# Two-layer hybrid encoder on one core: other buffers for the first feed-forward weights, block sums queued behind the last tile's eviction, row means on ScalarE

## The chip, the core and the metric

The kernel runs on one NeuronCore of a Trainium2 chip. The core has five engines with queues of their own: TensorE (PE, matrix products into PSUM), VectorE (DVE), ScalarE (ACT), GpSimd (POOL) and SyncE (SP, which here only issues transfers). The metric is the time of one execution in device microseconds, the median of several executions. The profile is one further execution with the hardware profiler on.

## The reference, cut to what matters

Two layers over 1024 tokens of width 1024, all in float32:

```python
for l in range(DEPTH):                       # DEPTH = 2
    h = _rmsnorm(x, g_pre_mix[l])
    z = h @ w_in[l]
    ...                                      # Fourier, windowed attention and memory groups -> y_f, y_a, y_m
    y = concat([rms(y_f), rms(y_a), rms(y_m)]) @ w_out[l]
    x = x + _rmsnorm(y, g_post_mix[l])
    h = _rmsnorm(x, g_pre_ffn[l])
    gate, up = jnp.split(h @ w_ffn_in[l], 2, axis=-1)      # D_FF = 2816
    f = (jax.nn.silu(gate) * up) @ w_ffn_out[l]
    x = x + _rmsnorm(f, g_post_ffn[l])
```

`_rmsnorm(x, g)` is `x * rsqrt(mean(x*x) + 1e-6) * g`, row by row.

## The kernel before, in words

**Products.** A float32 product is made of three products of split operands: `split` (L151, L152) rounds a block to a high part on ScalarE and takes the low part, source minus high part, on VectorE (or GpSimd); TensorE then multiplies high by high, high by low and low by high. Tokens are worked on in 8 tiles of 128 rows.

**The seam between attention and feed-forward.** The second half of the attention (`att_units(1)`), the output product and both norms are woven tile by tile in one loop over `i` (it runs to `NT + 4`). For tile `t`, `out` (L1030 to L1045) multiplies the tile by `w_out` (products `mo`, L162), evicts each half of 512 columns from PSUM on VectorE with the scale of its group (L1041), then calls `residual` and `norm_x`: the square with its row sum on ScalarE (L335), the row mean and its power -1/2 on GpSimd (L210, L212), scale and gain on VectorE (L337), the sum into `x` on VectorE (L338), then square (L289), mean and power on GpSimd again, and scale and gain on VectorE (L294). `Blocks.tile` transposes the normed tile on TensorE (`hTp`, L1066) and copies it out of PSUM on ScalarE (L1067).

**The feed-forward's first product** runs as one level of Strassen's scheme: seven block products, numbered 1 to 7, in the order 2, 4, 5, 1, 6, 7, 3. The token operands are blocks of 512 tokens by 512 columns, b11, b21 (tiles 0 to 3) and b12, b22 (tiles 4 to 7), and their sums: 2 and 4 need tiles 0 to 3 alone, the others tiles 4 to 7 as well. `Blocks.sum(n, c)` makes one quarter of the operand of product n: for 1, 4 and 6 a sum on VectorE (L1084), then in each case a split. `Blocks.last(c)` overwrites b21 and b12 with the sums (L1096, L1097) of which 7 and 3 are made. The weights come in quads: a `Quad` loads two blocks of `w_ffn_in` (512 KB each, L1112, on SP), `weights(i)` makes the operand of product i (for 1, 2, 5, 6 and 7 a sum on VectorE, L1127, then a split), and `step(i)` issues its 12 matmuls (L1137, results `qy`, `qz`, `qx`, `qw`) and the combinations. A gate quad and an up quad form a pair; there are 11 pairs in each layer. The steps of the first pair stand in the layer's loop, those of the others in `ffn_in`. Each layer ends with the second product `ffn_out` (`fo`, L1272), and the last tiles' norm.

**Buffers.** SBUF is two arenas, one for split operands and one for plain float32, with slots of 256 columns given by number. Rings of slot numbers (`qws` for quad weights, `sns` for copies of products, `wsums` for weight sums, `xfs` for the x and f of a tile) are reset at each seam. In the seam the x and f of tiles 5, 6 and 7 lie at 32 and 0, 16 and 20, 24 and 28, the attention's probabilities at 36 to 47, the two gains at 48 and 52.

**Order.** Each engine works through its queue in order. The order is fixed when the kernel is built: the framework goes through the instructions in the order in which the program names them and places them by a timeline model of its own, so that an instruction named later can be queued ahead of one that this model expects to wait. `tc.issue_after(ins)` makes every instruction in its block that runs on the engine of `ins` queue behind `ins`.

Of the kernel before, what the change touches and what calls it, by code (L numbers as in the profile page):

```python
# [15 lines left out]
AF = mybir.ActivationFunctionType  # L16
ALU = mybir.AluOpType
# [3 lines left out]
D = 1024  # L21
S = 1024
NT = S // P
# [3 lines left out]
FW = 256  # L27
# [7 lines left out]
EPS = 1e-6  # L35
# [31 lines left out]

@with_exitstack
def tile_encoder(ctx: ExitStack, tc: tile.TileContext, T, C, out):
    nc = tc.nc  # L70

# [10 lines left out]
    def nm(s):  # L82
        uid[0] += 1
        return f"{s}_{uid[0]}"
# [36 lines left out]
    def run(k, n, step):  # L121
        return Ring(*[k + i * step for i in range(n)])
# [7 lines left out]
    qws, sns, silus, acts = Ring(32, 0, 16, 20), Ring(36, 38, 40, 42, 32, 34), run(8, 5, 2), run(18, 7, 2)  # L130
    sums, wsums = run(8, 4, 2), Ring(4, 6)
# [6 lines left out]
    def sm(n, name="v"):  # L138
        if name not in smp:
            smp[name] = ctx.enter_context(tc.tile_pool(name="sm_" + name, bufs=N_SM.get(name, 4)))  # L140
        return smp[name].tile([P, n], F32, tag=name, name=nm(name))

    def ps(shape, name="ps", tag="pd"):
        return psp[tag].tile([P] + list(shape), F32, tag=tag, name=nm(name))
# [24 lines left out]
    def cst(*shape):  # L169
        n = math.prod(shape)  # L170
        ap = const[:, used[0] : used[0] + n]
        used[0] += -(-n // 8) * 8
        names = "abc"[: len(shape)]
        dims = {c: d for c, d in zip(names, shape)}
        return ap.rearrange(f"p ({' '.join(names)}) -> p {' '.join(names)}", **dims) if len(shape) > 1 else ap
# [4 lines left out]
    nc.vector.memset(ones, 1.0)  # L180
    mhalf = cst(8)
    nc.vector.memset(mhalf, -0.5)
    halfpi = cst(1)
    nc.vector.memset(halfpi, math.pi / 2)

# [4 lines left out]
        out=mask[:, 0:P], in_=mask[:, 0:P], pattern=[[1, P]], compare_op=ALU.is_ge,  # L190
# [4 lines left out]
        out=mask[:, 2 * P : 3 * P], in_=mask[:, 2 * P : 3 * P], pattern=[[-1, P]],  # L195
# [5 lines left out]
    rx = cst(NT)  # L201
# [2 lines left out]
    CC = cst(NT, HD // 2)  # L204
    SS = cst(NT, HD)

    def rsqrt_mean(ss, n, width, name="rs"):

        v = sm(width, name + "v")
        nc.gpsimd.tensor_scalar(out=v, in0=ss, scalar1=1.0 / n, scalar2=EPS, op0=ALU.mult, op1=ALU.add)  # L210
        r = sm(width, name)
        nc.gpsimd.tensor_tensor(out=r, in0=v, in1=mhalf[:, 0:width], op=ALU.pow)  # L212
        return r

    def gain(row, g):
# [70 lines left out]
    def norm_x(x, g, h=None, keep=None):  # L286

        ss = sm(1, "nss")
        nc.scalar.activation(junks(D // 2).bitcast(BF16) if h is None else h, x, AF.Square, accum_out=ss)  # L289
        if keep is not None:  # L290
            nc.scalar.dma_start(keep, x)
        h = x if h is None else h
        r = rsqrt_mean(ss, D, 1, "nrs")
        nc.vector.scalar_tensor_tensor(out=h, in0=x, scalar=r[:, 0:1], in1=g, op0=ALU.mult, op1=ALU.mult)  # L294
        return h

    def token_scale(x, t):

        ss = sm(1, "nss")
        nc.scalar.activation(junks(D // 2).bitcast(BF16), x, AF.Square, accum_out=ss)  # L300
        v = sm(1, "nrsv")
        nc.gpsimd.tensor_scalar(out=v, in0=ss, scalar1=1.0 / D, scalar2=EPS, op0=ALU.mult, op1=ALU.add)
        nc.gpsimd.tensor_tensor(out=rx[:, t : t + 1], in0=v, in1=mhalf[:, 0:1], op=ALU.pow)

    def norm_T(h, hT, t, tag="pd"):

# [13 lines left out]
    def residual_out(x, f, g, dst, t):  # L320

        ss = sm(1, "rss")
        nc.scalar.activation(junks(D // 2).bitcast(BF16), f, AF.Square, accum_out=ss)  # L323
        r = rsqrt_mean(ss, D, 1, "rrs")
        for n in range(2):
            ns = slice(n * 512, n * 512 + 512)
            nc.vector.scalar_tensor_tensor(out=f[:, ns], in0=f[:, ns], scalar=r[:, 0:1], in1=g[:, ns], op0=ALU.mult, op1=ALU.mult)
            (nc.gpsimd if t in (1, 3) else nc.vector).tensor_tensor(out=x[:, ns], in0=x[:, ns], in1=f[:, ns], op=ALU.add)
            (nc.sync, nc.scalar)[n].dma_start(dst[:, ns], x[:, ns])

    def residual(x, f, g, eng=None):

        junk = junks(D // 2).bitcast(BF16)
        ss = sm(1, "rss")
        nc.scalar.activation(junk, f, AF.Square, accum_out=ss)  # L335
        r = rsqrt_mean(ss, D, 1, "rrs")
        nc.vector.scalar_tensor_tensor(out=f, in0=f, scalar=r[:, 0:1], in1=g, op0=ALU.mult, op1=ALU.mult)  # L337
        (eng or nc.vector).tensor_tensor(out=x, in0=x, in1=f, op=ALU.add)  # L338

# [146 lines left out]
    class Mix:  # L486
# [57 lines left out]
        def fourier_units(self):  # L544

            v = nc.vector
# [18 lines left out]
            def products(r):  # L565
                th, tl, dh, dl = st.pop(("d", r))
                pt = ps([256], "yfp", "sc")
                acc = Acc(pt, 2)
                for i in range(2):
                    acc.add(th[:, i], tl[:, i], dh[:, i], dl[:, i])  # L570
                y = yfs(256)
                ss = sm(1, "fss")
                nc.scalar.activation(y, pt, AF.Square, accum_out=ss)
                rs = rsqrt_mean(ss, FW, 1, "frs")
                nc.scalar.activation(y, pt, AF.Copy, scale=rs[:, 0:1])
                st["y", r] = y

# [452 lines left out]
        def out(self, t, x1):  # L1030

            x, f = self.xf.pop(t)
            (hi, lo), rs = self.prepped.pop(t)
            for n in range(2):
                ns = slice(n * 512, n * 512 + 512)
                pt = ps([512], "mo")
                acc = Acc(pt, 4)
                for i in range(4):
                    w = self.woa[2 + i]
                    acc.add(hi[:, i], lo[:, i], w[0][:, ns], w[1][:, ns])  # L1040
                nc.vector.scalar_tensor_tensor(  # L1041
                    out=f[:, ns], in0=pt, scalar=rs[:, 0:1], in1=f[:, ns], op0=ALU.mult, op1=ALU.add
                )
            residual(x, f, self.gpost)
            return norm_x(x, self.gffn, f, x1)  # L1045
# [130 lines left out]
    def gate_out(q):  # L1176
        res = []
        for c in q.out:
            s = silus(512)
            nc.scalar.activation(s, c, AF.Silu)  # L1180
            res.append(s)
        return res
# [23 lines left out]
    def quads(l, p, hb):  # L1206
        return [Quad(l, j * DFF + 2 * p * P, hb) for j in range(2)]

    def ffn_in(l, hb, actd, first):

        for p in range(NFF // 2):
            if p == 0:
                gq, uq = first
                g = gate_out(gq)
                up_out(uq, g, actd, p)
                qws.ks, wsums.ks, sns.ks = (44, 48, 52, 56), (4, 6, 0, 2), (36, 38, 40, 42, 32, 34)
                continue
            gq, uq = quads(l, p, hb)
            for q in (gq, uq):
                q.load()  # L1220
                for i in ORDER:
                    q.step(i)
                if q is gq:
                    g = gate_out(gq)
            up_out(uq, g, actd, p)
# [121 lines left out]
    mix = Mix(0, hT, mem)  # L1347
# [13 lines left out]
    for l in range(DEPTH):  # L1361
# [4 lines left out]
        q = mix.skewed(mix.q, mix.q_turn, NT)  # L1366
# [8 lines left out]
        hb = Blocks()  # L1375
        hs = {}
        first = gq, uq = quads(l, 0, hb)
        qws.ks, wsums.ks, sns.ks = (32, 0, 16, 20), (4, 6), (36, 38, 40, 42, 56, 58)
        for r in (qws, wsums, xfs, sns, silus, acts, sums, wcs):
            r.i = 0  # L1380
        mix.values_32()
# [1 line left out]
        for i in range(NT + 4):  # L1383
            if i < NT + SKEW:
                att[i]()
            if 2 <= i < NT + 2:
                hs[i - 2] = mix.out(i - 2, x1d[i - 2])
            if i >= 4:
                hb.tile(hs.pop(i - 4), i - 4)
            if 1 <= i < NT + 1:  # L1390
                mix.out_rows(i - 1, xs[i - 1], pmd[i - 1])
            if 5 <= i < 9:
                hb.sum(2, i - 5)
            if i == NT + 1:
                gq.load()
                gq.step(2)
                for c in range(4):
                    hb.sum(4, c)
            if i == NT + 2:
                gq.step(4)  # L1400
                uq.load()
                uq.step(2)
                uq.step(4)
            if i > NT:
                for c in (i - NT - 1,) if i < NT + 3 else (2, 3):
                    hb.sum(5, c)
        for q in first:
            q.step(5)
        for n in (1, 6, 7, 3):
            for c in range(4):  # L1410
                hb.sum(n, c)
                if n == 6:
                    hb.last(c)
            for q in first:
                q.step(n)
        ffn_in(l, hb, actd, first)
# [4 lines left out]
        if l + 1 < DEPTH:  # L1421
            mem = Memory(l + 1, 16, 0, 16, 28, "pT")
            mix = Mix(l + 1, nhT, mem)
# [83 lines left out]
```

## Time and profile before

| | us |
|---|---|
| median of 3 runs | 2080.04 (2077.87 to 2081.79) |
| the profiled execution | 2080.67 |
| its span, first to last instruction | 2078.9 |
| PE busy | 1996.4 |
| DVE busy | 1572.7 |
| ACT busy | 1071.5 |
| POOL busy | 714.1 |
| mean granted TensorE clock | 0.981 of full speed |

A row of a group of instructions in the profile names the line, the engine, the operation, output and inputs by the program's names, partitions by elements and the count; behind the bar stand the busy time in us, the mean of one in ns, and the idle time of the engine in front of them with what ended it. A row of a timeline begins with start and length in us, and shows in brackets how long the engine was idle before and which engine's line ended that. In the chain of waits each row is start, length and what the end of the span waited for at that moment. Times within the span count from its start.

### The profile page before, as it was taken

How to read it: one execution, taken by the hardware profiler on the slowest of the kernel's cores; microseconds unless marked ns; L12 is line 12 of the kernel's file. 1: busy time of each engine (PE TensorE's matmuls, PEld its weight loads, DVE VectorE, ACT ScalarE, POOL GpSimd, SP SyncE). 2: the span in 40 equal slices, each digit the busy share in tenths (PEclk: the TensorE clock that was granted, in tenths of full speed). 3: DMA queues.
4: the chain of work that ended last, by engine and by line, in shares of the span. 5: the costliest groups of instructions: out<-in, count | busy, mean ns of one | idle time of the engine just before them, and what ended most of it. 6: DMA issues, size and time to landing. Idle time of an engine off the chain costs nothing.

```text
span 2078.9 us, 28540 instructions
## 1 busy us (share of the span) xinstructions
PE 1996.4 (96%) x9587; PEld 1646.8 (79%) x9587; DVE 1572.7 (76%) x2540; ACT 1071.5 (52%) x2270; POOL 714.1 (34%) x819
## 2 busy tenths in 40 slices
PE   7998999799999999999999989998999999999998
PEld 6876787588888888887888768876888888878886
DVE  5668767898787886768876687679887787778766
ACT  7467777554333333545555677686433333345451
POOL 5344445433333433002423544453442342320012
PEclk9999999899999999999999999998999999999999
DMA  6112132423232333879741122233233233269983
GB/s 222 45 48 67 61 102 96 158 67 106 96 115 94 115 103 115 304 267 327 273 153 49 57 67 77 78 123 130 97 117 101 87 132 97 97 210 342 302 274 141
DMA packets 173347, 286.48 MB, mean 138 GB/s; under 512 B 15464, under 2 KB 73360, under 8 KB 173200
## 3 DMA queue, kind: packets, MB, share of 16 engines
q1 hardware_dynamic: 165136, 265.78, 38.4%
q10 hardware_dynamic: 8064, 18.88, 2.4%
q8 instruction: 75, 1.23, 0.2%
q14 instruction: 72, 0.59, 0.1%
HBM read 218.02 MB, written 66.58 MB: 137 GB/s over the span
## 4 chain that ended last, share of the span: by engine, by line
PE 79%; DVE 7%; DMA 5%; ACT 3%; issue 2%; POOL 2%; SPq 0%; DVEq 0%; POOLq 0%; ACTq 0%
PE fo L1272 14%; PE qx L1137 11%; PE qz L1137 11%; PE qy L1137 11%; PE mo L162 7%; PE qw L1137 6%; PE kvp L162 4%; PE qp L162 3%; DVE arena_r L152 2%; DMA arena_f<-actd 2%; PE pT L798 2%; PE zT L162 2%; PE sc L761 2%; DMA arena_f<-in_w_ffn_out 1%; PE av L813 1%
## 5 line engine op out<-in xcount | busy, mean ns | idle before, releaser
L151 ACT CAST arena_r<-arena_f 128x512 fp32r<-128x512 f32 (+1 forms) x780 | 443.8, 591 | 646.4 <-PE qz L1137 114.0
L152 DVE TENSOR_TENSOR arena_r<-arena_f,arena_r 128x512 fp32r<-128x512 f32 (+1 forms) x676 | 509.4, 775 | 146.3 <-ACT arena_r L151 136.4
L1272 PE MATMUL fo<-arena_r 128*128 128x512 f32 x1848 | 426.5, 392 | 8.1 <-ACT arena_r L151 6.9
L1272 PEld LDWEIGHTS fo<-arena_r 128*128 128x128 f32 x1848 | 347.9, 189 | 82.0 <-ACT arena_r L151 5.7
L1137 PE MATMUL qy<-arena_r 128*128 128x512 f32 x1056 | 261.6, 397 | 21.4 <-ACT arena_r L151 15.3
L1137 PEld LDWEIGHTS qy<-arena_r 128*128 128x128 f32 x1056 | 201.3, 192 | 66.1 <-ACT arena_r L151 16.4
L1127 DVE TENSOR_TENSOR arena_f<-arena_f 128x512 f32<-128x512 f32 x220 | 201.3, 920 | 11.5 <-DMA arena_f<-in_w_ffn_in 6.7
L1137 PE MATMUL qz<-arena_r 128*128 128x512 f32 x704 | 195.7, 389 | 0.2 <-ACT arena_r L151 0.2
L1157 POOL TENSOR_TENSOR arena_f<-arena_f 128x512 f32<-128x512 f32 x44 | 74.5, 1695 | 318.0 <-ACT arena_f L1142 318.0
L1137 PEld LDWEIGHTS qz<-arena_r 128*128 128x128 f32 x704 | 132.1, 188 | 28.0 <-ACT arena_r L151 0.6
L152 POOL TENSOR_TENSOR arena_r<-arena_f,arena_r 128x256 fp32r<-128x256 f32 (+2 forms) x104 | 86.3, 837 | 123.0 <-ACT arena_r L151 88.7
L1137 PE MATMUL qw<-arena_r 128*128 128x512 f32 x528 | 127.3, 389 | 0.0
L1137 PE MATMUL qx<-arena_r 128*128 128x512 f32 x528 | 127.3, 389 | 0.0
L1137 PE MATMUL qx<-big,arena_r 128*128 128x512 f32 x528 | 127.0, 389 | 0.0
L1189 POOL TENSOR_TENSOR arena_f<-arena_f 128x512 f32<-128x512 f32 x40 | 66.2, 1655 | 170.5 <-DVE arena_f L1169 127.1
L1137 PEld LDWEIGHTS qx<-arena_r 128*128 128x128 f32 x528 | 99.1, 188 | 20.6
L1137 PEld LDWEIGHTS qx<-big,arena_r 128*128 128x128 f32 x528 | 99.1, 188 | 20.6
L1137 PEld LDWEIGHTS qw<-arena_r 128*128 128x128 f32 x528 | 99.1, 188 | 20.6
L1137 PE MATMUL qz<-big,arena_r 128*128 128x512 f32 x352 | 115.2, 389 | 0.0
L210 POOL TENSOR_SCALAR rrsv<-rss 128x1 f32<-128x1 f32 x32 | 15.7, 492 | 268.1 <-ACT arena_f L323 208.6
L162 PE MATMUL mo<-big,arena_r 128*128 128x512 f32 x384 | 104.1, 410 | 0.7 <-ACT arena_f L1001 0.4
L162 PE MATMUL mo<-arena_r 128*128 128x512 f32 x384 | 100.5, 402 | 0.4 <-ACT arena_f L1001 0.3
(228 smaller groups left out, 3520.0 us busy)
## 6 DMA issues: line engine op xcount, KB each, us to landing
arena_f<-in_w_ffn_out SPq DMA_DIRECT2D x264, 256.0 KB, 4.7
arena_f<-in_w_ffn_in SPq DMA_DIRECT2D x88, 512.0 KB, 3.6
actd<-arena_f SPq DMA_DIRECT2D x154, 256.0 KB, 3.7
arena_f<-actd SPq DMA_DIRECT2D x154, 256.0 KB, 4.6
arena_f<-in_w_in SPq DMA_DIRECT2D x40, 256.0 KB, 2.9
arena_f<-in_x SPq DMA_DIRECT2D x16, 512.0 KB, 4.9
arena_f<-in_w_out SPq DMA_DIRECT2D x32, 256.0 KB, 2.8
pmd<-arena_f ACTq DMA_DIRECT2D x32, 256.0 KB, 2.0
```

What stands on the lines that cost most here:

```text
L151: nc.scalar.copy(hi, src)
L152: return (lo_eng or nc.vector).tensor_tensor(out=lo, in0=src, in1=f32(hi), op=ALU.subtract)
L162: mm(self.dst, a, b, start=self.i == 0, stop=self.i == self.n - 1)
L210: nc.gpsimd.tensor_scalar(out=v, in0=ss, scalar1=1.0 / n, scalar2=EPS, op0=ALU.mult, op1=ALU.add)
L761: mm(pt, lhs, self.kst[g][i][:, k0 * P : k1 * P], start=i == 0, stop=i == 1)
L798: nc.tensor.transpose(pT[:, h, :], es_[h // 2][:, h % 2, j * P : j * P + P], ident)
L813: mm(av, lhs, p_, start=j == 0 and i == 0, stop=j == nk - 1 and i == 1)
L1127: nc.vector.tensor_tensor(out=s, in0=a, in1=b, op=op)
L1137: mm(pt, a, b, start=start and n == 0, stop=n == 11, skip_group_check=not start)
L1157: nc.gpsimd.tensor_tensor(out=self.v, in0=self.v, in1=self.s2, op=ALU.add)
L1189: (G if i in (0, 3) else V).tensor_tensor(out=a[i], in0=c, in1=g[i], op=ALU.mult)
L1272: mm(pt, ab[:, 0, x, sl], ab[:, 1, y], start=new and first and j == 0, stop=last and j == 2, skip_group_check=not new)
```

## The change

Three things are changed. The first is where and when the first pair's weights are loaded and used: the gate quad's into slots 36 and 40 (attention probabilities), one turn of the loop earlier, the up quad's into 32 and 0 (x and f of tile 5) instead of tile 6's 16 and 20; both quads' step 2 stand together, then both quads' step 4; the copies of products get other slots. The second is that the operand blocks for products 1, 6, 7 and 3 are queued, as far as VectorE is concerned, behind the eviction of the last tile's second half. The third is that the row mean (times 1/n, plus epsilon) is made on ScalarE, in place, with the bias from a constant column, where a GpSimd instruction made it; the power -1/2 stays on GpSimd. `group_scale`, whose mean is on VectorE (L960), is not changed.

```diff
-    def rsqrt_mean(ss, n, width, name="rs"):
+    def rsqrt_mean(ss, n, r):
 
-        v = sm(width, name + "v")
-        nc.gpsimd.tensor_scalar(out=v, in0=ss, scalar1=1.0 / n, scalar2=EPS, op0=ALU.mult, op1=ALU.add)
-        r = sm(width, name)
-        nc.gpsimd.tensor_tensor(out=r, in0=v, in1=mhalf[:, 0:width], op=ALU.pow)
+        nc.scalar.activation(ss, ss, AF.Identity, scale=1.0 / n, bias=eps[:, 0:1])
+        nc.gpsimd.tensor_tensor(out=r, in0=ss, in1=mhalf[:, 0:1], op=ALU.pow)
         return r
...
-                nc.vector.scalar_tensor_tensor(
+                self.evicted = nc.vector.scalar_tensor_tensor(
                     out=f[:, ns], in0=pt, scalar=rs[:, 0:1], in1=f[:, ns], op0=ALU.mult, op1=ALU.add
                 )
...
-                qws.ks, wsums.ks, sns.ks = (44, 48, 52, 56), (4, 6, 0, 2), (36, 38, 40, 42, 32, 34)
+                qws.ks, wsums.ks, sns.ks = (48, 52, 56, 44), (4, 6, 0, 2), (36, 38, 40, 42, 32, 34)
...
-        qws.ks, wsums.ks, sns.ks = (32, 0, 16, 20), (4, 6), (36, 38, 40, 42, 56, 58)
+        qws.ks, wsums.ks, sns.ks = (36, 40, 32, 0), (4, 6), (44, 46, 56, 58, 24, 26)
...
+            if i == NT:
+                gq.load()
             if i == NT + 1:
-                gq.load()
-                gq.step(2)
                 for c in range(4):
                     hb.sum(4, c)
+                uq.load()
+                for q in first:
+                    q.step(2)
             if i == NT + 2:
-                gq.step(4)
-                uq.load()
-                uq.step(2)
-                uq.step(4)
+                for q in first:
+                    q.step(4)
...
         for n in (1, 6, 7, 3):
-            for c in range(4):
-                hb.sum(n, c)
-                if n == 6:
-                    hb.last(c)
+            with tc.issue_after(mix.evicted.ins):
+                for c in range(4):
+                    hb.sum(n, c)
+                    if n == 6:
+                        hb.last(c)
             for q in first:
                 q.step(n)
```

`token_scale`, which had the two instructions written out, now calls `rsqrt_mean`; the other callers pass the result's buffer.

More of the change, by code (lines that the diff above doesn't have):

```diff
@@ L182, in tile_encoder @@
     nc.vector.memset(mhalf, -0.5)
+    eps = mhalf[:, 1:2]
+    nc.vector.memset(eps, EPS)
     halfpi = cst(1)
@@ L292, in norm_x @@
         h = x if h is None else h
-        r = rsqrt_mean(ss, D, 1, "nrs")
+        r = rsqrt_mean(ss, D, sm(1, "nrs"))
         nc.vector.scalar_tensor_tensor(out=h, in0=x, scalar=r[:, 0:1], in1=g, op0=ALU.mult, op1=ALU.mult)
@@ L300, in token_scale @@
         nc.scalar.activation(junks(D // 2).bitcast(BF16), x, AF.Square, accum_out=ss)
-        v = sm(1, "nrsv")
-        nc.gpsimd.tensor_scalar(out=v, in0=ss, scalar1=1.0 / D, scalar2=EPS, op0=ALU.mult, op1=ALU.add)
-        nc.gpsimd.tensor_tensor(out=rx[:, t : t + 1], in0=v, in1=mhalf[:, 0:1], op=ALU.pow)
+        rsqrt_mean(ss, D, rx[:, t : t + 1])
     def norm_T(h, hT, t, tag="pd"):
@@ L323, in residual_out @@
         nc.scalar.activation(junks(D // 2).bitcast(BF16), f, AF.Square, accum_out=ss)
-        r = rsqrt_mean(ss, D, 1, "rrs")
+        r = rsqrt_mean(ss, D, sm(1, "rrs"))
         for n in range(2):
@@ L335, in residual @@
         nc.scalar.activation(junk, f, AF.Square, accum_out=ss)
-        r = rsqrt_mean(ss, D, 1, "rrs")
+        r = rsqrt_mean(ss, D, sm(1, "rrs"))
         nc.vector.scalar_tensor_tensor(out=f, in0=f, scalar=r[:, 0:1], in1=g, op0=ALU.mult, op1=ALU.mult)
@@ L573, in products @@
                 nc.scalar.activation(y, pt, AF.Square, accum_out=ss)
-                rs = rsqrt_mean(ss, FW, 1, "frs")
+                rs = rsqrt_mean(ss, FW, sm(1, "frs"))
                 nc.scalar.activation(y, pt, AF.Copy, scale=rs[:, 0:1])
```

## The prediction

> **What bounds the kernel now.** I read the page first, then the busy time by windows, the TensorE timeline where its idle time sits, the chain of waits there, and last the VectorE timeline of the same place.
>
> ```profile
> span 2078.9 us, 28540 instructions
> PE 1996.4 (96%) x9587; PEld 1646.8 (79%) x9587; DVE 1572.7 (76%) x2540; ACT 1071.5 (52%) x2270; POOL 714.1 (34%) x819
> ```
>
> TensorE (PE) is busy for 96% of the span, so a gain must come from the places where it stands. Two of those are the stretches that the change touches: between tile 7's last output product and the step 5 products of the first pair of quads, once in each layer. The columns of the windows are length, then the busy time of PE, PEld, DVE, ACT and POOL, then the granted clock.
>
> ```profile
> core 0: us, PE busy (x) PEld busy (x) DVE busy (x) ACT busy (x) POOL busy (x), PEclk, DMA share, GB/s
> 392.40:421.65 29.25, 15.97 (x52) 11.78 (x53) 26.64 (x38) 14.33 (x27) 5.45 (x7) 0.71 0.33 108
> 397.63:443.25 45.62, 36.74 (x146) 29.38 (x147) 42.18 (x62) 27.72 (x49) 14.13 (x10) 0.83 0.21 70
> 421.65:451.60 29.95, 29.95 (x134) 24.80 (x133) 28.73 (x42) 17.48 (x31) 12.24 (x6) 1.00 0.09 27
> 1417.40:1442.50 25.10, 15.37 (x62) 11.44 (x60) 24.37 (x38) 14.89 (x28) 7.01 (x7) 0.73 0.47 157
> 1419.84:1466.20 46.36, 37.88 (x154) 29.58 (x155) 44.45 (x68) 28.38 (x51) 17.11 (x10) 0.85 0.24 79
> 1442.50:1475.90 33.40, 33.20 (x145) 26.95 (x144) 31.15 (x48) 20.30 (x37) 11.03 (x4) 1.00 0.06 18
> ```
>
> In the first and the fourth row PE works for barely 16 of 29 us and 15 of 25 us, at a granted clock of 0.71 and 0.73, while DVE is 91% and 97% busy. In the third row 134 matmuls take 29.95 us, 0.2235 us each: that is PE without waits.
>
> ```profile
> 386.62 5.71 PE L162 MATMUL mo<-arena_r 128*128 128x512 f32 x24
> 396.01 0.82 PE L1137 MATMUL qy<-arena_r 128*128 128x512 f32 x2 [3.68 <-ACT arena_r L151]
> 400.77 4.64 PE L1137 MATMUL qy<-arena_r 128*128 128x512 f32 x10 [3.93 <-DVE arena_r L152]
> 414.77 1.22 PE L1137 MATMUL qy<-arena_r 128*128 128x512 f32 x2 [4.69 <-ACT arena_r L151]
> 421.65 0.62 PE L1137 MATMUL qz<-arena_r 128*128 128x512 f32 x2
> ...
> 1417.36 1.03 PE L1066 MATMUL hTp<-const,arena_f 128*128 128x128 f32 x8
> 1425.31 1.22 PE L1137 MATMUL qy<-arena_r 128*128 128x512 f32 x2 [6.92 <-ACT arena_r L151]
> 1442.49 0.39 PE L1137 MATMUL qz<-arena_r 128*128 128x512 f32 x1
> ```
>
> The products of tile 7 (mo) end at 392.33. Steps 2 and 4 (qy) are what PE could do while tile 7 goes through its norms, but their operands come late three times (3.68, 3.93, 4.69 us), and step 5 (qz) starts at 421.65. In layer 1 the products end at 1417.4 and step 5 starts at 1442.5. The chain of waits says why:
>
> ```profile
> 388.48 3.34 POOL grs L962
> ...
> 397.72 0.67 DVE arena_f L1041
> ...
> 399.70 1.68 POOL rrsv L210
> ...
> 402.04 1.28 DVE arena_f L337
> ...
> 404.44 1.29 DVE arena_f L294
> ...
> 407.35 5.99 DMA arena_f<-in_w_ffn_in
> ...
> 1415.04 0.68 DVE arena_f L1084
> 1415.71 0.60 DVE big L1096
> ...
> 1418.11 0.67 DVE arena_r L152
> ...
> 1419.91 1.32 DVE arena_f L1041 x2
> ```
>
> Two things are late. Tile 7's eviction (L1041) runs at 397.72, 5.4 us after its product. And the up quad's weights land only at 413.3: their buffers belong to tile 6, whose norm (L294) runs at 404.44, and the load also stood in SP's queue behind another one, for a buffer of the gains, for 16.4 us:
>
> ```profile
> SPq L1112 <- DVE arena_f L337: 16.4, 1, 16.4
> ```
>
> **The change, part by part.** *Loads.* The gate quad's weights go to two buffers of the attention, free once tile 7's probabilities are transposed; the up quad's go to tile 5's x and f, a tile earlier than now. The gate quad's then land before PE has finished tile 7. The up quad's still wait for tile 5's transposes, in layer 1 until 1418.4 (the row at 1417.36), and land about 6 us later (5.99 above), while PE has the gate quad's 24 matmuls, 5.4 us. So the first and the third wait above (3.68 and 4.69 us; 6.92 in layer 1) lose their cause. With both quads' step 2 and 4 at hand, PE has 48 matmuls, 10.7 us at 0.2235, to run beside tile 7's norms. The loads are the same in number and size; only their place in SP's queue and the wait in front change. The next pair's loads still wait for the gains and for the first pair's sums, with a whole quad (7 products of 12 matmuls, 18.8 us) to cover the up one's; I cost them at nothing, and one landing's 6 us if the cover is gone.
>
> *The block sums.* Now DVE, which takes its instructions in a fixed order, runs sums of products 1, 6 and 3 in front of tile 7's eviction:
>
> ```profile
> 385.79 0.68 DVE L1084 TENSOR_TENSOR arena_f<-big,big 128x512 f32<-128x512 f32 x1
> 386.39 0.68 DVE L1096 TENSOR_TENSOR big<-big,big 128x512 f32<-128x512 f32 x1
> ...
> 388.92 0.68 DVE L1084 TENSOR_TENSOR arena_f<-big,big 128x512 f32<-128x512 f32 x1
> 389.52 0.68 DVE L1096 TENSOR_TENSOR big<-big,big 128x512 f32<-128x512 f32 x1
> 390.12 0.69 DVE L1084 TENSOR_TENSOR arena_f<-big,big 128x512 f32<-128x512 f32 x1
> ...
> 392.76 1.29 DVE L337 SCALAR_TENSOR_TENSOR arena_f<-arena_f,rrs 128x1024 f32<-128x1024 f32 x1 [1.35 <-POOL rrs L212]
> ...
> 396.43 0.69 DVE L1097 TENSOR_TENSOR big<-big,big 128x512 f32<-128x512 f32 x1
> ```
>
> That is six, and with up to three low halves (L152) of those sums nine, at 0.60 us from start to start: 5.4 us. The change queues them behind the eviction, which can then run right after its product, at 392.4 instead of 397.7. Only DVE's instructions are queued; ScalarE's casts are not. What waits for the moved work is PE at steps 1, 6, 7 and 3, and DVE has no room there: from the eviction to the last operand of step 3 it is busy 42.18 of 45.62 us. So most of the early start is given back. What can be dropped from that stretch is work for the next pair:
>
> ```profile
> L1127 DVE TENSOR_TENSOR arena_f<-arena_f 128x512 f32<-128x512 f32 x13 | 9.9, 770 | 0.7 <-DMA arena_f<-in_w_ffn_in 0.7
> L210 POOL TENSOR_SCALAR rrsv<-rss 128x1 f32<-128x1 f32 x32 | 15.7, 492 | 268.1 <-ACT arena_f L323 208.6 <-ACT arena_f L335 55.6 <-ACT es L779 2.6
> L212 POOL TENSOR_TENSOR rrs<-rrsv,const 128x1 f32<-128x1 f32 x32 | 22.2, 693 | 2.4
> L779 ACT ACTIVATE es<-es 128x4 f32<-128x4 f32 x32 | 6.2, 194 | 0.0
> L1180 ACT ACT_TABLE_LOAD x2 | 2.6, 1283 | 0.0
> ```
>
> The first row counts the weight sums in 397.63 to 443.25: 13, of which the first pair needs ten in all. Three at least are for the next pair, with three low halves 6 x 0.60 = 3.6 us that may come later.
>
> *Row means.* Of each mean's two GpSimd instructions the first (L210, 0.49 us on average, 1.68 in the chain above) becomes one on ScalarE, right behind the square there. No row shows Identity on 128x1; the nearest is L779, 0.19 us for 128x4. The bounds are 0.3 us saved on average (0.49 less 0.19) and 1.5 us saved where GpSimd was held up (1.68 less 0.19); a loss needs another instruction between square and mean on ScalarE, and the code puts none there. I take 1 us a layer on tile 7's path, and nothing elsewhere: ScalarE is busy 52%, and the kernel's last chain swaps one short instruction for another. The Trainium skill (ScalarE: Activation LUTs, What ACT_TABLE_LOAD costs) gives about 280 ns plus 0.83 ns an element for an ACTIVATE whose bias is a pointer; by it the instruction is an estimated 0.28 us, 0.09 more at some eight means on the path, and the sum below 9.0 instead of 9.7 us.
>
> *The sum, layer 0.* DVE's list starts at 392.4. It is 42.2 + 5.4 - 3.6 = 44.0 us, with 3.4 us of waits (45.62 - 42.18) less the 1 us of row means: it ends at 438.8, against 443.25. Step 3's 24 matmuls (5.4 us) end the pair at 444.2. Before, 132 matmuls from 421.65 end it at 451.2. Gain 7.0 us. *Layer 1.* The list started at 1419.84; the three instructions quoted in front of it (1415.04, 1415.71, 1418.11) let it start 1.8 us earlier, at 1418.0. It is 44.45 + 5.4 - 3.6 = 46.2 us, with 1.9 us of waits less 1, and I take off 1.2 us because seven instead of nine are moved there (four more stand before 1410): end 1463.9, pair end 1469.3, against 1442.5 + 29.5 = 1472.0. Gain 2.7 us. Together 9.7 us.
>
> The profiled execution took 2080.67 us (span 2078.9), 0.6 above the median of 2080.04. 2080.67 - 9.7 - 0.6 gives 2070 for the median.
>
> **The rivals.** *A: DVE takes it all back.* The order in each queue is fixed ahead of the run by the framework's own timeline model. If it still places the eviction late, or puts all 16 instructions for product 6 and its follow-ups (9.6 us) in front of that product's weights, PE gets its wait back before step 6. For it: DVE at 91 to 97%. Against it: 3.4 us of DVE's waits and three late loads have a cause that goes. The gain is below 4.2 us: 2076 to 2084. Chance 0.17.
>
> *B: slower, by GpSimd being shut out.* grs above took 3.34 us, and an average rrs takes 0.69; it ran while DVE had L1084 and L1096 back to back and ended when DVE paused. Moved behind the eviction, those sums now lie exactly beside the four such means of tiles 6 and 7. If each takes 3.34 us, that is 8 x 2.65 = 21.2 us on the path, less the 9.7: 2092. It decides from 1.9 us each (9.7 / 8 above 0.69). Against it: DVE's next step in the chain waits for that mean, so DVE pauses by itself. 2085 to 2092, chance 0.13. The Trainium skill (SBUF — State Buffer, SBUF: two separate sides) says that a DVE instruction with two SBUF inputs and a GpSimd instruction that reads SBUF lock each other out, the first to start going through to its end. The trace agrees that GpSimd is shut out, but here over some five DVE instructions, not one.
>
> *C: DVE does not bind.* If its remaining work fits beside PE, the pair ends at 392.4 + 168 x 0.2235 + 16 transposes of 0.13 = 432.0 in layer 0 (19.2 us earlier) and, with 24 transposes, at 1458.1 in layer 1 (13.9): 2047, and partly so up to 2062. Against it are the busy rows. Chance 0.13.
>
> *D: table loads.* If Identity needed a table of its own, each mean would cost up to two loads of 1.283 us. Square and Copy already run here between Exp and Silu without one, so I give it 0.01, beyond the range. The Trainium skill (ScalarE: Activation LUTs, Table sets: the hidden batching unit) says that every set has identity.
>
> **How the numbers follow.** About 0.2%, 4.2 us, is what a measurement of this kernel can tell from no change. Forecast 2063 to 2076: 0.56; A 0.17; B 0.13; C 0.13; D 0.01. Faster is the forecast and C, 0.69; same is A, 0.17; slower is B and D, 0.14. The range of 2056 to 2082 leaves out B and D, the far half of C and the upper edge of A.
>
> **What would show it.** In the changed profile: qy starts within 1 us of the last mo and its three waits of 3.7 to 4.7 us are gone; L1041 of tile 7 follows its product within 1 us; L337 and L294 of tile 7 come 5 us earlier in layer 0; no L1084, L1096 or L1097 of these products ahead of that L1041; a new wait of PE on DVE or ACT at qw (step 6), 5 us or so; L210 gone from POOL, as many short instructions more on ACT, and no table load more. I am wrong if PE runs through step 6 without a wait (C), or if the means of tiles 6 and 7 take over 1.9 us each on POOL (B).

## The result, and the profile after

The changed kernel takes 2096.56 us in the median (2095.17 to 2100.11, 4 runs), where the kernel before took 2080.05 beside it (2077.87 to 2081.79, 4 runs). The ratio is 1.0084, 95% interval 1.0069 to 1.0099: slower by 16.5 us or so, where 10 us faster was forecast. The first lines of its page:

```profile
span 2093.4 us, 28489 instructions
...
PE 2007.2 (96%) x9587; PEld 1653.7 (79%) x9587; DVE 1585.7 (76%) x2541; ACT 1088.9 (52%) x2354; POOL 692.6 (33%) x735
```

The 84 means have gone from POOL (819 to 735 instructions) to ACT (2270 to 2354). The span is 14.5 us longer, of which 10.8 are in PE's busy time (1996.4 before) although its matmuls are as many, at a mean granted clock of 0.974 instead of 0.981.

**The seam in layer 0.** TensorE's timeline of the changed kernel, between tile 7's product and step 6:

```profile
389.50 4.60 PE L162 MATMUL mo<-arena_r 128*128 128x512 f32 x19
...
394.98 3.00 PE L1135 MATMUL qy<-arena_r 128*128 128x512 f32 x12
398.95 3.04 PE L1135 MATMUL qy<-arena_r 128*128 128x512 f32 x12 [0.98 <-ACT arena_f L1140]
403.41 0.73 PE L1135 MATMUL qy<-arena_r 128*128 128x512 f32 x2 [1.42 <-ACT arena_r L151]
407.36 1.09 PE L1064 MATMUL hTp<-const,arena_f 128*128 128x128 f32 x4 [3.22 <-DVE arena_f L294]
...
419.21 0.73 PE L1135 MATMUL qz<-arena_r 128*128 128x512 f32 x2 [1.90 <-ACT arena_r L151]
421.62 0.88 PE L1135 MATMUL qx<-arena_r 128*128 128x512 f32 x2 [1.68 <-ACT arena_r L151]
...
433.82 5.60 PE L1135 MATMUL qw<-arena_r 128*128 128x512 f32 x24
```

Lines behind some 300 are two lower than before (L1137 is now L1135, L1041 L1039). The three waits of 3.68, 3.93 and 4.69 us at qy are down to 0.98 and 1.42, the way that was forecast. New ones stand at the transposes (3.22, for the last step of tile 6's norm) and at the first products of step 5 (1.90 and 1.68), and none at step 6. VectorE and GpSimd of the same place:

```profile
395.79 0.75 DVE L1039 SCALAR_TENSOR_TENSOR arena_f<-mo,grs,arena_f 128x512 f32<-128x512 f32 x1
396.45 0.69 DVE L1082 TENSOR_TENSOR arena_f<-big,big 128x512 f32<-128x512 f32 x1
...
402.93 1.28 DVE L335 SCALAR_TENSOR_TENSOR arena_f<-arena_f,rrs 128x1024 f32<-128x1024 f32 x1 [0.44 <-POOL rrs L212]
...
414.81 1.29 DVE L294 SCALAR_TENSOR_TENSOR arena_f<-arena_f,nrs 128x1024 f32<-128x1024 f32 x1 [0.44 <-POOL nrs L212]
```

```profile
398.51 4.39 POOL L212 TENSOR_TENSOR rrs<-rss,const 128x1 f32<-128x1 f32 x1 [5.42 <-ACT rss L211]
402.93 0.55 POOL L212 TENSOR_TENSOR nrs<-nss,const 128x1 f32<-128x1 f32 x1
411.52 3.26 POOL L212 TENSOR_TENSOR nrs<-nss,const 128x1 f32<-128x1 f32 x1 [8.05 <-ACT nss L211]
```

Tile 7's eviction starts at 395.79, 1.7 us after its product ended at 394.10, where 5.4 us lay between them before. But its last norm step (L294) starts only at 414.81, 19 us behind the eviction. Before, it stood 11.3 us behind:

```profile
408.98 1.28 DVE L294 SCALAR_TENSOR_TENSOR arena_f<-arena_f,nrs 128x1024 f32<-128x1024 f32 x1 [0.80 <-POOL nrs L212]
```

In the changed kernel two powers of a 128x1 column took 4.39 and 3.26 us, each to the moment when VectorE had nothing left to start; the one between them took 0.55, though VectorE's L335 started at the same moment.

**Where the time went.** The lengths of the stages, in us, each between the starts of two of TensorE's rows (last mo to first fo, and so on). "Control" is the kernel before held in its own order, a run told of below, and shows how far two profiles of one order differ:

| stage | before | control | after |
|---|---|---|---|
| start to layer 0's last mo | 391.9 | 397.1 | 393.7 |
| to its first fo (seam and feed-forward) | 440.5 | 440.4 | 438.0 |
| to its last fo | 233.5 | 232.6 | 234.7 |
| to layer 1's first qz (its attention, start of its seam) | 376.6 | 378.0 | 390.0 |
| to its first fo | 411.5 | 411.5 | 412.0 |
| to its last fo | 215.9 | 216.8 | 216.1 |

The seam of layer 0 is 2.5 us shorter. The loss of 12 to 13 us is in one stage, most of it in an attention that no line of the change names (the means of its Fourier rows apart).

### The profile page after: what moved, and what is told of

Read it like the earlier page. It is cut to its first block, busy times and chain, and to the rows that moved or that the text cites. A ratio compares the mean times of both kernels' runs of the same rounds, so it can differ in the third digit from the quotient of the medians.

```text
span 2093.4 us, 28489 instructions
## 1 busy us (share of the span) xinstructions
PE 2007.2 (96%) x9587; PEld 1653.7 (79%) x9587; DVE 1585.7 (76%) x2541; ACT 1088.9 (52%) x2354; POOL 692.6 (33%) x735
## 4 chain that ended last, share of the span: by engine, by line
PE 81%; DVE 6%; ACT 4%; DMA 4%; issue 3%; POOL 2%; SPq 0%; DVEq 0%; POOLq 0%; ACTq 0%
PE fo L1270 16%; PE qz L1135 11%; PE qx L1135 11%; PE qy L1135 11%; PE mo L162 7%; PE qw L1135 6%; PE kvp L162 4%; PE qp L162 3%; DVE arena_r L152 2%; PE zT L162 2%; PE sc L759 2%; PE pT L796 2%; ACT arena_r L151 1%; DMA arena_f<-in_w_in 1%; PE av L811 1%
## 5 line engine op out<-in xcount | busy, mean ns | idle before, releaser
L1135 PE MATMUL qy<-arena_r 128*128 128x512 f32 x1056 | 257.9, 393 | 5.3 <-ACT arena_r L151 3.8
L1135 PEld LDWEIGHTS qy<-arena_r 128*128 128x128 f32 x1056 | 200.0, 190 | 49.0 <-ACT arena_r L151 4.7
L1125 DVE TENSOR_TENSOR arena_f<-arena_f 128x512 f32<-128x512 f32 x220 | 209.1, 953 | 9.1 <-DMA arena_f<-in_w_ffn_in 4.0
L1135 PE MATMUL qz<-arena_r 128*128 128x512 f32 x704 | 199.5, 396 | 4.6 <-ACT arena_r L151 3.6
L1135 PEld LDWEIGHTS qz<-arena_r 128*128 128x128 f32 x704 | 134.3, 192 | 34.7 <-ACT arena_r L151 4.2
L1135 PE MATMUL qx<-arena_r 128*128 128x512 f32 x528 | 128.0, 391 | 1.8 <-ACT arena_r L151 1.8
L1135 PE MATMUL qw<-arena_r 128*128 128x512 f32 x528 | 126.7, 389 | 0.0
L1135 PE MATMUL qx<-big,arena_r 128*128 128x512 f32 x528 | 126.5, 389 | 0.0
L1135 PEld LDWEIGHTS qx<-arena_r 128*128 128x128 f32 x528 | 99.2, 188 | 23.4 <-ACT arena_r L151 3.0
L1135 PEld LDWEIGHTS qw<-arena_r 128*128 128x128 f32 x528 | 99.1, 188 | 20.6
L1135 PEld LDWEIGHTS qx<-big,arena_r 128*128 128x128 f32 x528 | 99.1, 188 | 20.6
L212 POOL TENSOR_TENSOR rrs<-rss,const 128x1 f32<-128x1 f32 x32 | 25.9, 809 | 270.4 <-ACT rss L211 269.4
L1135 PE MATMUL qz<-big,arena_r 128*128 128x512 f32 x352 | 115.2, 389 | 0.0
```

Source lines behind the costliest of these rows:

```text
L212: nc.gpsimd.tensor_tensor(out=r, in0=ss, in1=mhalf[:, 0:1], op=ALU.pow)
L1125: nc.vector.tensor_tensor(out=s, in0=a, in1=b, op=op)
L1135: mm(pt, a, b, start=start and n == 0, stop=n == 11, skip_group_check=not start)
```

## The experiments

All ratios are of runs against runs of the kernel before on the same chip, with 95% intervals; 0.1% is 2.1 us. Four came first, which divide the change.

**Row means alone** (the first hunk of the change, nothing else). 

> The kernel before with the row means on ScalarE and nothing else changed. Theory 1 (the loss outside the seams, 12 us in the changed kernel, comes with the row means, which alter the fixed order of the queues in the whole program): slower by 6 to 14 us, with layer 1's last attention product 6 us or more later. Theory 2 (the loss comes from the seam, whose new order carries over into layer 1): within 3 us of before.

Measured 1.0046 (1.0032 to 1.0061), about 9 us slower.

**Loads and queueing alone** (all but the first hunk, means on GpSimd). 

> The kernel before with the loads and the queueing of the block sums, the row means left on GpSimd. Theory 1: within 5 us of before, layer 0 up to its last attention product exactly as before. Theory 2: slower by 8 us or more, most of it in layer 1's attention.

Measured 1.0010 (0.9994 to 1.0027).

**Loads alone** (that without `issue_after`). 

> The loads, their order and the slots alone, the block sums queued as the framework likes. If the loads are what helps and the queueing costs, by means of tiles 6 and 7 held up on GpSimd: faster than before by 3 to 10 us and faster than the seam as a whole. If the queueing is what helps: no faster than before.

Measured 1.0047 (1.0031 to 1.0064).

**Queueing alone** (the kernel before with `issue_after`).

```diff
-            for c in range(4):
-                hb.sum(n, c)
...
+            with tc.issue_after(mix.evicted.ins):
+                for c in range(4):
+                    hb.sum(n, c)
```

> The queueing of the block sums alone, loads as before. If the sums behind the eviction hold up the means on GpSimd: slower than before by 2 to 8 us, with a power instruction of 3 us or more after tile 7's eviction in each layer. If they free the chain as I forecast: faster by 2 to 6 us.

Measured 1.0013 (0.9997 to 1.0028).

The first two runs come out as theory 1 has them. The loads alone are "no faster than before", as the second of their theories has it, but neither theory gives a reason for 9 us more. The queueing alone, 2.7 us over before, is not clear of zero. The means cost 9 us, the seam's two edits nothing, all three 16.5: the parts do not add. The loads alone cost 9 us, and with the queueing nothing, though these two programs have the same instructions: `issue_after` only says which stands behind which. That points at the order of the queues. The framework works that order out anew for every program; between the kernel before and the one with the means alone, 4923 of 15532 instructions stand at another place in their engine's queue, 2944 of them in TensorE's, which makes no mean.

**Order and means apart.** The next four hold an order: every instruction gets an edge to the one that a list puts ahead of it in its queue (order only, no wait for its end).

```diff
         tile_encoder(tc, T, C, out)
+        hold(tc, nc)
...
+def hold(tc, nc):
...
+                tc.add_manual_dep(
+                    traced[k], last.name,
+                    mybir.DependencyInfo(mybir.DependencyClass.NoSync, mybir.DependencyReason.DATA), reason="hold",
+                )
```

> The row means on ScalarE alone, with every other instruction of the five engines held in the order of the kernel before (each mean directly behind its square on ScalarE). Theory D (the means cost by themselves: 84 more ScalarE instructions of 0.28 us, the path from square to power): about +9 us, 2089 to 2093 beside a before of 2080 to 2084, as in the run of the means alone. Theory O (the means cost only because the framework orders all five queues anew when they change): within 3 us of before.

Measured 1.0021 (1.0006 to 1.0035).

> The kernel before with its means on GpSimd, but with all instructions held in the order of the run of the means alone (each GpSimd mean directly ahead of its power). Theory D: within 3 us of before. Theory O: about +9 us, as in the run of the means alone. If both have a part, this run and the one with the old order divide the 9 us between them.

Measured 1.0067 (1.0050 to 1.0084).

> The whole change, held in the order of the run with the loads and the queueing alone (the seam run, which took the time of before). Theory D: 2092 to 2098, as the changed kernel (16.5 us over before). Theory O: within 3 us of before, so the 16.5 us are the order's.

Measured 1.0023 (1.0011 to 1.0036).

> The loads and the queueing alone, means on GpSimd, held in the order of the changed kernel. Theory D: within 3 us of before, as the seam run in its own order. Theory O: 12 to 17 us over before, as the changed kernel.

Measured 1.0058 (1.0035 to 1.0081).

The slow orders are slow with the means on GpSimd too, and the change in a good order is within 5 us of before. The two runs in good orders are 4.4 and 4.8 us over before, somewhat more than theory O's 3. So theory O holds for most of it: about 12 of the 16.5 us (0.58 of 0.84%) come with the order alone. The windows of the stage from layer 0's last fo to layer 1's first qz, one row of each kernel (length, then PE, PEld, DVE, ACT, POOL, granted clock). Before, and the control:

```profile
1065.90:1442.50 376.60, 353.01 (x1919) 288.62 (x1917) 273.65 (x576) 255.78 (x638) 164.19 (x265) 0.96 0.26 87
```

```profile
1070.10:1448.10 378.00, 352.61 (x1919) 288.77 (x1917) 274.93 (x578) 255.74 (x638) 163.94 (x265) 0.97 0.26 86
```

The new order with the means on GpSimd, and with the means on ScalarE (the run of the means alone):

```profile
1068.40:1458.10 389.70, 358.52 (x1930) 292.72 (x1929) 282.75 (x583) 258.24 (x641) 168.14 (x265) 0.96 0.25 84
```

```profile
1069.20:1456.10 386.90, 357.04 (x1931) 291.47 (x1930) 282.32 (x583) 264.49 (x673) 157.51 (x233) 0.96 0.25 84
```

The changed kernel, and its order with the means on GpSimd:

```profile
1066.40:1456.40 390.00, 360.32 (x1931) 293.63 (x1929) 284.82 (x586) 264.77 (x675) 157.82 (x233) 0.95 0.25 82
```

```profile
1066.10:1457.20 391.10, 358.70 (x1931) 291.62 (x1929) 284.72 (x585) 258.29 (x643) 168.05 (x265) 0.96 0.25 82
```

Length less PE's busy time is TensorE's idle time: 23.6 and 25.4 us in the old order, 31.2 and 29.9 in the new one, 29.7 and 32.4 in the changed kernel's. Within these pairs, who makes the means does not show. Of the new order's other 5.5 us (358.52 less 353.01 of PE's busy time), 2.5 are eleven matmuls that lay in the next stage before (411.5 us there, 408.8 in the new order, so this part is no loss), and 3 are matmuls that took longer. TensorE's longest waits in the middle of the stage (1205 to 1265; line it waited for, us in total, times, longest), before and in the new order with the means on GpSimd:

```profile
PE mpT L895 <- POOL arena_f L885: 4.0, 4, 3.0
PE ms L873 <- ACT arena_f L879: 2.1, 1, 2.1
PE mav L906 <- ACT arena_r L151: 1.6, 1, 1.6
```

```profile
PE mav L906 <- ACT arena_r L151: 4.1, 3, 3.0
PE ms L873 <- ACT arena_f L879: 2.4, 1, 2.4
PE mpT L895 <- POOL arena_f L885: 2.0, 1, 2.0
PE mav L906 <- DVE arena_r L152: 1.2, 1, 1.2
PE qT L743 <- DVE arena_r L407: 1.0, 1, 1.0
```

Of the kinds that come to 1 us or more, 7.7 us by three have become 10.7 us by five; with the smaller ones it is 9.6 and 12.1 us. No single wait stands out, and no instruction is new.

In the old order the same stage does differ by who makes the means. With them on ScalarE it took 385.20 us, 7.2 more than the control:

```profile
1065.60:1450.80 385.20, 355.80 (x1919) 290.30 (x1917) 275.11 (x578) 264.10 (x670) 156.31 (x233) 0.96 0.25 85
```

In the seam order, two profiles with them on ScalarE have 383.8 and 384.9 us here, and the one with them on GpSimd 379.9. The times of whole executions, further down, do not bear out a difference of that size.

**Which part of the order, and does holding cost.**

> The kernel before, nothing changed, held in its own order. If holding costs nothing: within 2 us of before, and the 0.21% of the means in the old order are the means'. If the 0.21% are the holding's: 3 to 6 us over before here too.

Measured 1.0010 (0.9998 to 1.0022): holding costs nothing that can be told.

> The kernel before in its own order, but layer 1's attention (from its memory product to near the end of the mixing product) in the order of the run of the means alone: 1584 of the 4923 instructions that stand elsewhere there. Theory L1 (the cost is this stage's: in the traces it took 10 to 11 us longer in the new order, whoever made the means): 8 to 12 us over before. Theory E (the cost is spread, or the seam gives it back): 0 to 5 us over before.

Measured 1.0042 (1.0028 to 1.0056).

> The complement: the order of the run of the means alone everywhere but in layer 1's attention, which keeps the old one. Theory L1: 1 to 5 us over before (layer 0 ended 2.5 us later in the new order). Theory E: 8 to 14 us over before.

Measured 1.0042 (1.0030 to 1.0055).

> The kernel before with the order of the queueing run up to the middle of layer 0's last product (342 instructions stand elsewhere), and the old order behind it. In the queueing run layer 0 ended 4.3 us earlier than before and layer 1 gave it back. If the stages add: 2 to 4 us faster than before. If what a later stage takes depends on what came ahead of it: within 2 us of before.

Measured 0.9990 (0.9978 to 1.0002).

About 9 us each for the two halves of the new order: the first run has theory L1's number and the second theory E's, so neither theory holds for both. Layer 1's attention has half of the cost, layer 0 with the seams the other half, and the sum (0.84%) is near the whole (0.67%). The profile of the new order with the means on GpSimd had put most of it in layer 1. The last of the four, a splice of two orders, is the fastest kernel of the study by its mean ratio, but its interval takes in 1: not shown to beat the kernel before.

**What the means themselves cost.**

> The row means on ScalarE except the 16 of the Fourier rows (tile frs), which stay on GpSimd; everything held in the order of the kernel before. The run with all means and the old order was 0.21% over before. Theory F (that rest is the Fourier means: each lies between a square and a copy on ScalarE while ScalarE is the busiest queue, and layer 1's wait at yfT grew from 2.55 to 3.40 us with a slower TensorE clock behind it): within 2 us of before, or up to 2 us faster from the seams. Theory S (every mean costs ScalarE time on the path): 3 to 4 us over before, 68/84 of it.

Measured 1.0010 (0.9996 to 1.0025).

> Only the 16 Fourier means on ScalarE, everything else as in the kernel before and held in its order. Theory F: 3 to 5 us over before, as the run with all means. Theory S: within 1.5 us of before, 16/84 of it.

Measured 1.0013 (1.0001 to 1.0025).

> The whole change but with the 16 Fourier means on GpSimd, held in the order of the run of the loads and the queueing alone. The same with all means on ScalarE was 0.23% over before, with layer 0 ending 2 us earlier than in the seam run and layer 1 losing 4 us up to its query product. Theory F: 0 to 4 us faster than before, the gain of layer 0 kept. Theory S: 2 to 5 us over before.

Measured 1.0012 (0.9998 to 1.0027).

These two theories are not told apart: all three lie at the control's 1.0010. ScalarE's timeline shows what there is to find. Before, in layer 1's Fourier rows, and with the means on ScalarE in the same order:

```profile
1151.74 0.19 ACT L573 ACTIVATION_READ_ACCUMULATOR arena_f<-yfp 128x1 f32 x1
1151.84 0.61 ACT L151 CAST arena_r<-arena_f 128x512 fp32r<-128x512 f32 x1
```

```profile
1151.58 0.19 ACT L571 ACTIVATION_READ_ACCUMULATOR arena_f<-yfp 128x1 f32 x1
1151.81 0.29 ACT L211 ACTIVATE fss<-fss,const 128x1 f32<-128x1 f32 x1
1152.01 0.60 ACT L151 CAST arena_r<-arena_f 128x512 fp32r<-128x512 f32 x1
```

A mean takes 0.29 us and puts off what is behind it by 0.33 (0.43 from read to cast instead of 0.10). In times of whole executions, over four orders, the step from GpSimd to ScalarE was +0.11% (old order, against the control), +0.13 and 0.00% (seam order, two runs), -0.21% (new order) and +0.26% (the changed kernel's): both signs, no pair of intervals apart. In the changed kernel some 5 us are left beside the order's 12; that they are the means' is not shown. What the traces do show of the means is a longer wait in layer 1's Fourier stage, told in the last section.

**Why the seam gave nothing.** Tile 7's last norm step stood behind ten sums and splits. In two of the next three runs it is moved up in VectorE's queue, all else held. These are rows of that queue in layer 0; layer 1 is alike:

```diff
 L1095 TENSOR_TENSOR big<-big,big
+L294 SCALAR_TENSOR_TENSOR arena_f<-arena_f,nrs
 L152 TENSOR_TENSOR arena_r<-arena_f,arena_r
...
 L1125 TENSOR_TENSOR arena_f<-arena_f
-L294 SCALAR_TENSOR_TENSOR arena_f<-arena_f,nrs
```

> The whole change in the order of the seam run, but in VectorE's queue tile 7's last norm step (L294) stands six places earlier in layer 0 and four in layer 1 (four and five instructions are left between it and the step before). Theory Q (the line ahead of the norm and the GpSimd power held behind it are what ate the forecast gain): L294 starts about 3.4 us earlier in layer 0 and 2.3 in layer 1, the wait of TensorE at tile 7's transposes (8.2 us in layer 0) shrinks by as much, and the time falls by 3 to 6 us against the unmoved order. Theory V (VectorE's total work binds, as it was 91 to 97% busy): the wait moves to the operands of products 1 and 6, and the time is within 1.5 us of the unmoved order.

Measured 1.0015 (1.0002 to 1.0028).

> The unmoved order, the same program as the whole change held in the order of the seam run, beside the others on this chip: 0.1 to 0.35% over before, as it was.

Measured 1.0010 (0.9999 to 1.0021).

> The loads and the queueing with the means on GpSimd, in their own order but for the same move of L294 in both layers. Its own order took 0.10% over before. Theory Q: 3 to 6 us less than that, so 1 to 4 us faster than before. Theory V: within 1.5 us of its own order, 0 to 4 us over before.

Measured 1.0019 (1.0008 to 1.0030).

Theory V holds: nothing is gained. TensorE's and GpSimd's timelines of layer 0 show it, first in the unmoved order (the first of its two runs):

```profile
414.30 1.94 PE L1064 MATMUL hTp<-const,arena_f 128*128 128x128 f32 x8 [8.18 <-DVE arena_f L294]
418.39 1.22 PE L1135 MATMUL qz<-arena_r 128*128 128x512 f32 x2 [2.15 <-ACT arena_r L151]
```

```profile
408.20 4.63 POOL L212 TENSOR_TENSOR nrs<-nss,const 128x1 f32<-128x1 f32 x1 [7.94 <-ACT nss L211]
```

Then with the step moved up:

```profile
406.47 1.66 PE L1064 MATMUL hTp<-const,arena_f 128*128 128x128 f32 x8 [4.48 <-DVE arena_f L294]
414.26 1.22 PE L1135 MATMUL qz<-arena_r 128*128 128x512 f32 x2 [6.13 <-ACT arena_r L151]
```

```profile
404.06 1.03 POOL L212 TENSOR_TENSOR nrs<-nss,const 128x1 f32<-128x1 f32 x1 [7.93 <-ACT nss L211]
```

The transposes wait 3.7 us less (8.18 to 4.48), GpSimd's power is 3.6 us shorter, and the first product of step 5 waits 4.0 us more (2.15 to 6.13): it starts 26.3 us after tile 7's last mo in both (392.1 and 388.0).

## Why the prediction was wrong, step by step

- *Loads.* The mechanism was right. The three waits in layer 0 shrank to 0.98 and 1.42, and the 6.92 us of layer 1 to 2.39. What it left out is that in layer 1 a weight sum of the first pair stands in VectorE's queue ahead of the eviction and waits 1.29 us for its load. The eviction came 3.2 us after its last product (1427.28), not at once:

```profile
1429.91 0.69 DVE L1125 TENSOR_TENSOR arena_f<-arena_f 128x512 f32<-128x512 f32 x1 [1.29 <-DMA arena_f<-in_w_ffn_in]
1430.52 1.40 DVE L1039 SCALAR_TENSOR_TENSOR arena_f<-mo,grs,arena_f 128x512 f32<-128x512 f32 x2
```

- *Block sums.* The eviction was to start right after its product; it started 1.7 us behind in layer 0. The sums went behind it, and so ahead of tile 7's norm.
- *The sum for the seam.* "Gain 7.0" was 2.5 us in layer 0 (1.3 with the means left on GpSimd), and "gain 2.7" was none in layer 1 (436.9 us from mo to fo before, 437.0 in the seam run, 441.5 in the changed kernel). In layer 0 step 5 did get about the forecast lead: it started 25.5 us after tile 7's last mo instead of 29.7, with all 48 matmuls of steps 2 and 4 done instead of 36. But the sum took 0.2235 us for each matmul behind it, and step 5's 48 took 14.61 us, where the first 48 from step 5's start took 10.75 before. In them lie a wait of 1.68 us and slower work, at a granted clock of 0.88 instead of 1.00. The windows of the changed kernel and of before:

```profile
419.21:433.82 14.61, 12.93 (x48) 10.07 (x49) 13.42 (x22) 9.44 (x17) 4.96 (x2) 0.88 0.00 1
```

```profile
421.65:432.40 10.75, 10.75 (x49) 8.91 (x48) 9.56 (x17) 7.93 (x14) 4.24 (x1) 1.00 0.01 2
```

  The step that failed: an earlier eviction and earlier loads were counted as an earlier end of VectorE's list, with TensorE at full speed behind it. Up to step 5's operands that list is the bound, as rival A had it; the run with the norm step moved shows a wait of 4 us go from one of TensorE's rows to the next.
- *Rival B.* Two of the four powers of tiles 6 and 7 in layer 0 met its price: 4.39 and 3.26 us, over the 1.9 from which it was to decide. It still did not decide, since 3.6 us less of it bought nothing. The Trainium skill (SBUF — State Buffer, SBUF: two separate sides) says that a GpSimd instruction that reads SBUF and a VectorE instruction with two SBUF inputs lock each other out for one whole instruction. The trace agrees that GpSimd is shut out, but here over a row of such instructions.
- *Rival C* was to be known by step 6 without a wait. There was none (433.82), yet C was not the case: the waits stood at the transposes and at step 5.
- *Row means.* "A loss needs another instruction between square and mean on ScalarE, and the code puts none there": the queue did. In layer 1 two casts stand between, 0.93 us:

```profile
1445.35 0.19 ACT L289 ACTIVATION_READ_ACCUMULATOR arena_f<-arena_f 128x1 f32 x1
1445.44 0.61 ACT L151 CAST arena_r<-big 128x512 fp32r<-128x512 f32 x1
1445.95 0.62 ACT L151 CAST arena_r<-arena_f 128x512 fp32r<-128x512 f32 x1
1446.47 0.29 ACT L211 ACTIVATE nss<-nss,const 128x1 f32<-128x1 f32 x1
```

- *The step that set the sign* is "and nothing elsewhere". Rival A knew that the order in each queue "is fixed ahead of the run by the framework's own timeline model", and used it for the seam alone. Swapping 84 short instructions between engines gave all five queues another order, and such an order costs 12 to 14 us with no mean moved. None of the rivals had that, and the range ended below it.
- *Rival D* was rightly put at next to nothing: the table loads stayed at six.

What stays open is which of the swaps inside the new order costs most (half lies in layer 1's attention), why the framework's model came to it, and whether the means cost a few us of their own. That the loads alone cost 9 us and nothing with the queueing is put down to the order because their instructions are the same; the two orders were not exchanged piece by piece.

## What to carry to other kernels

Where a framework works out the queues, an edit is two changes: what it says, and a new order everywhere; here the second was worth 0.4 to 0.7%, more than any of the three edits. Compare the orders before reading the traces, and test the edit with the old order held: here such runs told the two apart to within 5 us. And where one engine's list was the bound, an earlier start of one of its steps moved a wait and removed none.

## What the runs showed of the hardware that was not expected

A power of a 128x1 column on GpSimd, 0.55 us by itself, took 4.63 us beside seven VectorE instructions run back to back (the unmoved order, above). It ended at 412.83, 0.4 us after the last of them:

```profile
411.74 0.68 DVE L1125 TENSOR_TENSOR arena_f<-arena_f 128x512 f32<-128x512 f32 x1
```

With the norm step moved up, it started as the last instruction ahead of that step did, and took 1.03. Waits also went with slower work behind them. TensorE's timeline in layer 1's Fourier stage, and its window behind the wait, before:

```profile
1167.25 0.44 PE L582 MATMUL yfT<-const,arena_f 128*128 128x128 f32 x2 [2.55 <-ACT arena_f L575]
...
1168.80 6.91 PE L162 MATMUL qp<-big,arena_r 128*128 128x512 f32 x24
```

```profile
1168.00:1183.00 15.00, 14.88 (x67) 12.39 (x67) 10.92 (x21) 4.14 (x11) 5.42 (x8) 0.89 0.00 1
```

And with the means on ScalarE in the same order:

```profile
1168.87 0.44 PE L580 MATMUL yfT<-const,arena_f 128*128 128x128 f32 x2 [3.40 <-ACT arena_f L573]
...
1171.68 8.20 PE L162 MATMUL qp<-big,arena_r 128*128 128x512 f32 x24 [0.71 <-ACT arena_f L582]
```

```profile
1170.00:1185.00 15.00, 14.15 (x55) 11.04 (x55) 8.48 (x15) 3.16 (x8) 5.40 (x8) 0.77 0.01 1
```

The wait grew by 0.85 us and a second one of 0.71 came; the 24 matmuls behind took 1.29 us more, at a granted clock of 0.77 instead of 0.89 over these 15 us. The longer wait comes back in all five profiles with these means on ScalarE in the old or the seam order: 3.38 to 3.84 us, each with the second of 0.71, against 2.39 to 2.89 us in the ten that have them on GpSimd and the same 24 matmuls behind. The 24 matmuls took 7.29 to 8.20 us in the five and 5.74 to 7.36 in the ten. That is longer as a rule, but the two groups touch, so how much of it is the wait's price is not shown.
